# Overlapping windows copied by DMA alone: twelve staged batches in place of eleven, and packets of twice the size

## The chip, the cores and the metric

The kernel runs on one core of a Trainium2 chip. The metric is the device time of one execution in microseconds (us). A few repeated executions of the kernel before give its spread; one further execution was recorded by the hardware profiler.

## The reference

```python
batch, length, dim = (32, 4096, 256)     # float32
window_size, stride = 64, 32
n_windows = (length - window_size) // stride + 1      # 127
for i in range(n_windows):
    result[:, i] = x[:, i * stride : i * stride + window_size]
```

Nothing is computed: the result is a copy. Cut each batch of `x` into 128 blocks of 32 rows; a block is 32 x 256 x 4 = 32,768 bytes. Window `w` of a batch is block `w` followed by block `w+1`, 65,536 bytes in all. So every block but the first and the last of a batch appears twice in the result: as the first half of window `w` and as the second half of window `w-1`. The input has 134.2 MB, the result 32 x 127 x 65,536 bytes = 266.3 MB.

## The kernel before, in words

No compute engine does any work. There are two ways for a window to get into the result.

**Direct.** `Copier.windows` (L42 to L57, the DMA at L48) copies whole windows from DRAM to DRAM. Overlapping blocks are read twice. `max_dma_last_dim` sets the size of one packet: 32,768 bytes (`DIRECT`), so a window is two packets. With `half` 0 or 1 the DMA copies only the first or the second half of each of its windows.

**Staged.** `Copier.load` (DMA at L60) brings a whole batch, 128 blocks, into an SBUF tile of 128 partitions, one block each. `Copier.store` (DMA at L72) writes the tile twice: as the first halves and as the second halves of the windows. Here a block is read from DRAM once and written twice. Packets are 16,384 bytes (`IN`, `OUT`). A batch has 128 blocks but only 127 windows, so each of the two stores has one block too many; it lands in the half window next door, in the neighbouring batch, and that window is written again later. The last staged batch (number 30) avoids this by storing in four DMAs, of 112, 15, 15 and 112 rows (L99).

Three queues feed the same DMA engines:

- **ACT's queue** (`ring_s`) carries the staged batches 1, 4, ..., 28 and 30, eleven in all. `Staging.run` (L109 to L116) issues six loads into six tiles, then twelve stores, then five loads, then the last stores. A load into a used tile waits for both stores of that tile.
- **SP's queue** (`ring_d`) carries 7 groups of 16 windows, 112 windows, of each of the 21 other batches (L171 to L183). A counter (`share`, `turns`) decides for each group whether it goes as one DMA of whole windows or as two DMAs of halves.
- **GpSimd's queue** (`ring_r`, called POOL in the profile) carries the remaining 15 windows of each direct batch, among them those that a staged neighbour spills into. It starts when the group marked `near`, the third from the end of SP's list, has landed (L187), and waits for the stores of each neighbour before its DMA (L189 to L192).

At the end SP waits for all three (L193 to L195). A DMA tells its semaphore of the landing through packets of 4 bytes; these are records of their own in the trace.

Of the kernel before, what the change touches and what calls it, by code (L numbers as in the profile page):

```python
# [6 lines left out]


DIRECT, IN, OUT = 32768, 16384, 16384
PIECES = (32768,)  # L10


class Copier:


    def __init__(self, nc, tc, x, out, B, L, D, W, S, n_win):
        assert W == 2 * S and L % S == 0
        self.nc, self.tc, self.x, self.out = nc, tc, x, out
        self.B = B
        self.blk = S * D  # L20
        self.nb = L // S
        self.nw = n_win
        self.total = 0
        self.done = tc.alloc_semaphore("done")
        self.last = tc.alloc_semaphore("last")
        self.last_total = 0

    def xap(self, block, dims):
        return bass.AP(self.x.tensor, self.x.offset + block * self.blk, dims)

    def oap(self, elem, dims):
        return bass.AP(self.out.tensor, self.out.offset + elem, dims)

    def count(self, dma):
        dma.then_inc(self.done, 16)
        self.total += 16

    def count_last(self, dma):
        dma.then_inc(self.last, 16)
        self.last_total += 16  # L40

    def windows(self, q, b, w0, n, half=None, piece=DIRECT, count=None):  # L42

        blk = self.blk
        size = 2 * blk if half is None else blk
        off = blk if half else 0
        (count or self.count)(
            q.dma_start(  # L48
                out=self.oap((b * self.nw + w0) * 2 * blk + off, [[2 * blk, n], [1, size]]),
                in_=bass.AP(  # L50
                    self.x.tensor,
                    self.x.offset + (b * self.nb + w0) * blk + off,
                    [[blk, n], [1, size]],
                ),
                max_dma_last_dim=piece,
            )
        )  # L57

    def load(self, q, t, b):
        return q.dma_start(  # L60
            out=t[:, :], in_=self.xap(b * self.nb, [[self.blk, self.nb], [1, self.blk]]),
            max_dma_last_dim=IN,
        )

    def store(self, q, t, b, half, p0=0, n=None):

        blk = self.blk
        n = self.nb if n is None else n  # L70
        w = b * self.nw + p0 - half
        return q.dma_start(  # L72
            out=self.oap(w * 2 * blk + half * blk, [[2 * blk, n], [1, blk]]),
            in_=t[p0 : p0 + n, :],
            max_dma_last_dim=OUT,
        )


class Staging:


    def __init__(self, c, pool, dtype, batches, bufs):
        self.c, self.batches = c, batches
        self.tiles = [pool.tile([128, c.blk], dtype, name=f"xb{i}") for i in range(bufs)]
        self.loaded = [c.tc.alloc_semaphore(f"loaded{i}") for i in range(bufs)]
        self.stored = [c.tc.alloc_semaphore(f"stored{i}") for i in range(bufs)]

    def load(self, q, g):
        n, i = divmod(g, len(self.tiles))
        if n:  # L90
            q.wait_ge(self.stored[i], 32 * n)
        self.c.load(q, self.tiles[i], self.batches[g]).then_inc(self.loaded[i], 16)

    def store(self, q, g):
        n, i = divmod(g, len(self.tiles))
        q.wait_ge(self.loaded[i], 16 * (n + 1))
        if g == len(self.batches) - 1:

            for half, p0, rows in ((0, 0, 112), (0, 112, 15), (1, 1, 15), (1, 16, 112)):  # L99
                self.c.count_last(self.c.store(q, self.tiles[i], self.batches[g], half, p0, rows))  # L100
            return
        for half in (0, 1):
            self.c.store(q, self.tiles[i], self.batches[g], half).then_inc(self.stored[i], 16)

    def wait_stored(self, q, g):
        n, i = divmod(g, len(self.tiles))
# [12 lines left out]
@with_exitstack  # L119
def kernel(  # L120
    ctx: ExitStack,
    tc: tile.TileContext,
    x: bass.AP,
    window_size: bass.AP,
    stride: bass.AP,
    out: bass.AP,
):
    nc = tc.nc
    W, S = int(window_size), int(stride)
    B, L, D = x.shape  # L130
    n_win = (L - W) // S + 1
    assert out.shape == (B, n_win, W, D)
    c = Copier(nc, tc, x, out, B, L, D, W, S, n_win)
    staged = [*range(1, B - 3, 3), B - 2]
    direct = [b for b in range(B) if b not in staged]
    pool = ctx.enter_context(tc.tile_pool(name="xb", bufs=1))
    st = Staging(c, pool, x.dtype, staged, 6)
    ring_d, ring_s = nc.sync, nc.scalar
    spilled = staged[:-1]

    waits = {b: [g for g, n in enumerate(spilled) if abs(n - b) == 1] for b in direct}
    per, loads, stores = 6, 6 * 17, 34

    def first(b):
        return 0 if b - 1 not in spilled else 8 if len(waits[b]) == 2 else 15

    def rest_parts(b):
        if len(waits[b]) == 2:
            return [(0, 8), (120, 7)]
        return [(0 if b - 1 in spilled else 112, 15)]  # L150

    soft = tc.alloc_semaphore("soft")
    soft_total = 0

    near = tc.alloc_semaphore("near")

    def mark(dma):
        dma.then_inc(near, 16)

    def count_soft(dma):  # L160
        nonlocal soft_total
        dma.then_inc(soft, 16)
        soft_total += 16

    with tc.tile_critical():  # L165
        st.run(ring_s)

        turns = share = 0
        rests = []
        todo = 7 * len(direct)  # L170
        for b in direct:  # L171
            for j in range(7):
                at = turns % (loads + per * stores)
                share += 9 if at < loads else 3
                if share >= 12:
                    share -= 12
                    turns += 4
                    c.windows(ring_d, b, first(b) + 16 * j, 16, 0)
                    c.windows(ring_d, b, first(b) + 16 * j, 16, 1, count=mark if todo == 3 else None)
                else:  # L180
                    turns += 3
                    c.windows(ring_d, b, first(b) + 16 * j, 16, count=mark if todo == 3 else None)
                todo -= 1  # L183
            rests.append(b)

        ring_r = nc.gpsimd
        ring_r.wait_ge(near, 16)  # L187
        for i, b in enumerate(sorted(rests, key=lambda b: max(waits[b], default=0))):
            for g in waits[b]:  # L189
                st.wait_stored(ring_r, g)  # L190
            for w, n in rest_parts(b):
                c.windows(ring_r, b, w, n, None, PIECES[i % 1], count_soft)  # L192
        ring_d.wait_ge(c.done, c.total)  # L193
        ring_d.wait_ge(soft, soft_total)
        ring_d.wait_ge(c.last, c.last_total)  # L195


# [33 lines left out]
```

## Time and profile before

| | |
|---|---|
| median of 10 executions | 755.43 us (754.38 to 757.5) |
| profiled execution, its own time | 755.94 us |
| span of the profiled execution | 754.2 us |
| data moved by the DMA engines | 313.16 MB in 18,092 packets |
| DRAM read / written | 220.92 MB / 266.99 MB |
| SP's queue (q1) | 8,080 packets, 154.15 MB |
| ACT's queue (q10) | 9,002 packets, 138.35 MB |
| POOL's queue (q0) | 1,008 packets, 20.65 MB |

The span is the time between the first and the last instruction that the profiler saw on the core. The bytes of the DMA engines count each packet once; the DRAM bytes count what is read and what is written, so a direct packet counts in both and a staged one in one of them. The DMA share of a stretch is the mean busy share of the core's 16 DMA engines; it can be slightly above 1, because an engine's next packet starts a few ns before the last one's end. "Start" and "took" of every packet stand in the trace, with its queue and size, but not the engine that moved it.

### The profile page before, as it was taken

The page shows a single profiled execution, that of the slowest core. Times are in us where ns is not written, and L with a number is a line of the kernel's source. Part 1 is how long each engine was busy: PE and PEld are TensorE (multiplying, and loading weights), DVE is VectorE, ACT ScalarE, POOL GpSimd, SP SyncE. Part 2 cuts the span into 40 slices and gives each one's busy share as a digit, 9 for nine tenths or more (in the row PEclk, how much of TensorE's full clock was granted, in tenths as well). Part 3 has the DMA queues.
Part 4 walks back from the last instruction along what each step waited for, and adds up shares of the span by engine and source line. Part 5 has one row for each costly group of instructions (what it writes and reads, how often), then busy time and mean ns, then how long its engine had stood idle before and what let it go on. Part 6 is the DMA issues. An engine that isn't in the chain of part 4 may idle for free.

```text
span 754.2 us, 321 instructions
## 1 busy us (share of the span) xinstructions
POOL 12.4 (2%) x25
## 2 busy tenths in 40 slices
POOL 0000000000000000000000000000000000050000
DMA  9999999999999999999999999999999999999995
GB/s 370 422 426 416 428 423 418 432 421 417 424 424 417 410 428 414 421 420 420 428 423 398 428 422 428 433 421 434 424 427 423 417 423 423 421 425 423 407 411 220
DMA packets 18092, 313.16 MB, mean 415 GB/s; under 512 B 4312, under 2 KB 4312, under 8 KB 4312
## 3 DMA queue, kind: packets, MB, share of 16 engines
q1 hardware_dynamic: 8080, 154.15, 48.5%
q10 hardware_dynamic: 9002, 138.35, 44.0%
q0 software_dynamic: 1008, 20.65, 6.8%
q14 instruction: 2, 0.02, 0.0%
HBM read 220.92 MB, written 266.99 MB: 647 GB/s over the span
## 4 chain that ended last, share of the span: by engine, by line
another core or an unknown queue 91%; POOL 2%; issue 0%; POOLq 0%; SPq 0%
POOL out_dram L48 2%; POOLq L226 0%; SPq L165 0%; POOLq L107 0%
## 5 line engine op out<-in xcount | busy, mean ns | idle before, releaser
L48 POOL DMA_DIRECT2D out_dram<-in_x_dram x21 | 12.2, 586 | 683.6 <-DMA out_dram<-in_x_dram 662.4
L212 POOL MEMSET const-float32-0.0<- 128x1 f32 x1 | 0.1, 93 | 0.2 <-issue 0.2
L212 POOL MEMSET const-bfloat16-1.0<- 128x1 bf16 x1 | 0.1, 96 | 0.0
L212 POOL MEMSET const-float32-1.0<- 128x1 f32 x1 | 0.1, 93 | 0.0
L212 POOL MEMSET const-uint8-127<- 128x1 uint8 x1 | 0.1, 93 | 0.0
## 6 DMA issues: line engine op xcount, KB each, us to landing
out_dram<-in_x_dram SPq DMA_DIRECT2D x83, 1024.0 KB, 98.3
out_dram<-xb ACTq DMA_DIRECT2D x20, 4096.0 KB, 140.1
out_dram<-in_x_dram SPq DMA_DIRECT2D x128, 512.0 KB, 92.1
xb<-in_x_dram ACTq DMA_DIRECT2D x11, 4096.0 KB, 126.2
out_dram<-in_x_dram POOLq DMA_DIRECT2D x21, 960.0 KB, 46.5
out_dram<-xb ACTq DMA_DIRECT2D x2, 3584.0 KB, 127.7
out_dram<-xb ACTq DMA_DIRECT2D x2, 480.0 KB, 113.7
```

What stands on the lines that cost most here:

```text
L48: q.dma_start(out=self.oap((b * self.nw + w0) * 2 * blk + off, [[2 * blk, n], [1, size]]), in_=bass.AP(self.x.tensor, self.x.offset + (b * ...
L212: nc = _bacc.Bacc("TRN2", target_bir_lowering=False, num_devices=1)
```

## The change

- Packets are twice as large: 65,536 bytes direct (a window is one packet) and 32,768 bytes through SBUF (a block is one packet).
- Twelve batches are staged in place of eleven, 0, 3, 6, 9, 11, 14, 17, 20, 22, 25, 28 and 31, and 20 are direct. All stores have 128 partitions. Batch 0 is loaded one block later (blocks 1 to 128) and batch 31 one block earlier, so that their spilled halves fall into a direct neighbour and not outside the result. The first half of the first window of batch 0 and the second half of the last window of batch 31, which this leaves out, are two small direct DMAs with packets of 2,048 bytes.
- Direct groups are always whole windows. About every eleventh DMA on SP's queue has 32 windows in place of 16.
- On POOL's queue the remainders of 19 direct batches come in parts of 15, or of 8 and 7, windows. Of the last direct batch (30) come 4 windows, then 9 windows by `columns`, which cuts each block into 8 pieces of 4,096 bytes so that every one of 16 engines gets the same. Two more windows go by `columns` on SP's queue after the last staged batch has been stored.

```diff
-DIRECT, IN, OUT = 32768, 16384, 16384
-PIECES = (32768,)
+DIRECT, IN, OUT = 65536, 32768, 32768
...
+    def columns(self, q, b, w0, n):
+
+        part = self.blk // 8
+        row = [1, part]
+        return q.dma_start(
+            out=self.oap((b * self.nw + w0) * 2, [[part, 16], [2 * self.blk, n], row]),
+            in_=self.xap(b * self.nb + w0, [[part, 16], [self.blk, n], row]),
+        )
...
-        if g == len(self.batches) - 1:
-
-            for half, p0, rows in ((0, 0, 112), (0, 112, 15), (1, 1, 15), (1, 16, 112)):
-                self.c.count_last(self.c.store(q, self.tiles[i], self.batches[g], half, p0, rows))
-            return
         for half in (0, 1):
-            self.c.store(q, self.tiles[i], self.batches[g], half).then_inc(self.stored[i], 16)
+            self.c.store(q, self.tiles[i], self.batches[g], half, self.shift(g)).then_inc(self.stored[i], 16)
...
-    staged = [*range(1, B - 3, 3), B - 2]
+    staged = [0, 3, 6, 9, 11, 14, 17, 20, 22, 25, 28, 31]
...
+    st = Staging(c, tc, pool, x.dtype, staged, 6, {0: -1, B - 1: 1})
...
-        turns = share = 0
-        rests = []
-        todo = 7 * len(direct)
         for b in direct:
-            for j in range(7):
-                at = turns % (loads + per * stores)
-                share += 9 if at < loads else 3
-                if share >= 12:
-                    share -= 12
-                    turns += 4
-                    c.windows(ring_d, b, first(b) + 16 * j, 16, 0)
-                    c.windows(ring_d, b, first(b) + 16 * j, 16, 1, count=mark if todo == 3 else None)
-                else:
-                    turns += 3
-                    c.windows(ring_d, b, first(b) + 16 * j, 16, count=mark if todo == 3 else None)
-                todo -= 1
-            rests.append(b)
-
-        ring_r = nc.gpsimd
+            w = 0 if b - 1 not in staged else 8 if b + 1 in staged and b + 1 < B - 1 else 15
+            wend = w + 112
+            while w < wend:
+                share += 11
+                n = 16
+                if share >= 120 and w + 32 <= wend:
+                    share -= 120
+                    n = 32
+                todo -= n // 16
+                count(c.windows(ring_d, b, w, n), near if todo in (2, 2 - n // 16 + 1) and total[near] == 0 else done)
+                w += n
+                if todo <= 7 and not singles:
+                    singles = True
+                    count(c.windows(ring_d, B - 1, c.nw - 1, 1, 1, 2048), done)
+                    if 0 in staged:
+                        count(c.windows(ring_d, 0, 0, 1, 0, 2048), done)
+
         ring_r.wait_ge(near, 16)
...
+        for i, b in enumerate(direct[:-1]):
+            for g, n in enumerate(staged):
+                if abs(n - b) == 1:
+                    st.wait_stored(ring_r, g)
+            parts = [(0, 15)] if b - 1 in staged else [(112, 15)]
+            if b - 1 in staged and b + 1 in staged:
+                parts = [(0, 8), (120, 7)]
+            for w, n in parts:
+                count(c.windows(ring_r, b, w, n, None, pieces[i % len(pieces)]), rest)
+
+
+        count(c.windows(ring_r, last, 112, 4), rest)
+        count(c.columns(ring_r, last, 116, 9), rest)
+        st.wait_stored(ring_d, len(staged) - 1)
+        count(c.columns(ring_d, last, 125, 2), done)
+        for sem in (done, near, rest):
+            ring_d.wait_ge(sem, total[sem])
```

Built, the changed kernel has 132 DMAs on SP's queue (before 211), 36 on ACT's (35) and 23 on POOL's (21).

More of the change, by code (lines that the diff above doesn't have):

```diff
@@ L6, with __init__ @@
 from concourse._compat import with_exitstack
-DIRECT, IN, OUT = 32768, 16384, 16384
-PIECES = (32768,)
+DIRECT, IN, OUT = 65536, 32768, 32768
 class Copier:
-    def __init__(self, nc, tc, x, out, B, L, D, W, S, n_win):
+    def __init__(self, x, out, B, L, D, W, S, n_win):
         assert W == 2 * S and L % S == 0
-        self.nc, self.tc, self.x, self.out = nc, tc, x, out
+        self.x, self.out = x, out
         self.B = B
@@ L22, in __init__ @@
         self.nw = n_win
[L23 to L26, printed above, removed]
     def xap(self, block, dims):
         return bass.AP(self.x.tensor, self.x.offset + block * self.blk, dims)
[L31 to L40, printed above, removed]
@@ L42, in windows @@
-    def windows(self, q, b, w0, n, half=None, piece=DIRECT, count=None):
-        blk = self.blk
[L45 to L56, printed above, removed]
-        )
@@ L59, in load, with oap, windows @@
-    def load(self, q, t, b):
+    def oap(self, half_window, dims):
+        return bass.AP(self.out.tensor, self.out.offset + half_window * self.blk, dims)
+    def windows(self, q, b, w0, n, half=None, piece=DIRECT):
+        blk = self.blk
+        row = [1, 2 * blk if half is None else blk]
+        h = half or 0
+        return q.dma_start(
+            out=self.oap((b * self.nw + w0) * 2 + h, [[2 * blk, n], row]),
+            in_=self.xap(b * self.nb + w0 + h, [[blk, n], row]),
+            max_dma_last_dim=piece,
+        )
@@ L60, in load @@
+    def columns(self, q, b, w0, n):
+        part = self.blk // 8
+        row = [1, part]
         return q.dma_start(
-            out=t[:, :], in_=self.xap(b * self.nb, [[self.blk, self.nb], [1, self.blk]]),
+            out=self.oap((b * self.nw + w0) * 2, [[part, 16], [2 * self.blk, n], row]),
+            in_=self.xap(b * self.nb + w0, [[part, 16], [self.blk, n], row]),
+        )
+    def load(self, q, t, b, shift):
+        return q.dma_start(
+            out=t[:, :],
+            in_=self.xap(b * self.nb - shift, [[self.blk, self.nb], [1, self.blk]]),
@@ L62, in load, with store @@
             max_dma_last_dim=IN,
         )
[L65 to L71, printed above, removed]
+    def store(self, q, t, b, half, shift):
+        w = b * self.nw - half - shift
         return q.dma_start(
-            out=self.oap(w * 2 * blk + half * blk, [[2 * blk, n], [1, blk]]),
-            in_=t[p0 : p0 + n, :],
+            out=self.oap(2 * w + half, [[2 * self.blk, self.nb], [1, self.blk]]),
+            in_=t[:, :],
@@ L79, with __init__, shift @@
 class Staging:
-    def __init__(self, c, pool, dtype, batches, bufs):
-        self.c, self.batches = c, batches
+    def __init__(self, c, tc, pool, dtype, batches, bufs, shifts):
+        self.c, self.batches, self.shifts = c, batches, shifts
         self.tiles = [pool.tile([128, c.blk], dtype, name=f"xb{i}") for i in range(bufs)]
-        self.loaded = [c.tc.alloc_semaphore(f"loaded{i}") for i in range(bufs)]
-        self.stored = [c.tc.alloc_semaphore(f"stored{i}") for i in range(bufs)]
+        self.loaded = [tc.alloc_semaphore(f"loaded{i}") for i in range(bufs)]
+        self.stored = [tc.alloc_semaphore(f"stored{i}") for i in range(bufs)]
+    def shift(self, g):
+        return self.shifts.get(self.batches[g], 0)
     def load(self, q, g):
@@ L91, in load @@
             q.wait_ge(self.stored[i], 32 * n)
-        self.c.load(q, self.tiles[i], self.batches[g]).then_inc(self.loaded[i], 16)
+        self.c.load(q, self.tiles[i], self.batches[g], self.shift(g)).then_inc(self.loaded[i], 16)
     def store(self, q, g):
@@ L132 @@
     assert out.shape == (B, n_win, W, D)
-    c = Copier(nc, tc, x, out, B, L, D, W, S, n_win)
-    staged = [*range(1, B - 3, 3), B - 2]
+    c = Copier(x, out, B, L, D, W, S, n_win)
+    staged = [0, 3, 6, 9, 11, 14, 17, 20, 22, 25, 28, 31]
     direct = [b for b in range(B) if b not in staged]
     pool = ctx.enter_context(tc.tile_pool(name="xb", bufs=1))
[L137 to L153, printed above, removed]
-    near = tc.alloc_semaphore("near")
[L157 to L163, printed above, removed]
+    st = Staging(c, tc, pool, x.dtype, staged, 6, {0: -1, B - 1: 1})
@@ L165, with count @@
+    ring_d, ring_s, ring_r = nc.sync, nc.scalar, nc.gpsimd
+    done = tc.alloc_semaphore("done")
+    near = tc.alloc_semaphore("near")
+    rest = tc.alloc_semaphore("rest")
+    total = {done: 0, near: 0, rest: 0}
+    def count(dma, sem):
+        dma.then_inc(sem, 16)
+        total[sem] += 16
+    todo = 7 * len(direct)
+    share, singles = 0, False
     with tc.tile_critical():
         st.run(ring_s)
-        turns = share = 0
-        rests = []
-        todo = 7 * len(direct)
         for b in direct:
-            for j in range(7):
-                at = turns % (loads + per * stores)
-                share += 9 if at < loads else 3
-                if share >= 12:
-                    share -= 12
-                    turns += 4
-                    c.windows(ring_d, b, first(b) + 16 * j, 16, 0)
-                    c.windows(ring_d, b, first(b) + 16 * j, 16, 1, count=mark if todo == 3 else None)
-                else:
-                    turns += 3
-                    c.windows(ring_d, b, first(b) + 16 * j, 16, count=mark if todo == 3 else None)
-                todo -= 1
-            rests.append(b)
@@ L186 @@
-        ring_r = nc.gpsimd
-        ring_r.wait_ge(near, 16)
[L188 to L195, printed above, removed]
+            w = 0 if b - 1 not in staged else 8 if b + 1 in staged and b + 1 < B - 1 else 15
@@ new lines @@
+        ring_r.wait_ge(near, 16)
+        pieces = (65536,)
+        last = B - 2
+        for i, b in enumerate(direct[:-1]):
[7 more added lines that the diff above has]
+                count(c.windows(ring_r, b, w, n, None, pieces[i % len(pieces)]), rest)
```

## The prediction

> **What bounds the kernel now.** The page first: no engine computes, so its slices and the DMA queues are all there is. A packet of 4 bytes is the count towards a semaphore.
>
> ```profile
> DMA  9999999999999999999999999999999999999995
> DMA packets 18092, 313.16 MB, mean 415 GB/s; under 512 B 4312, under 2 KB 4312, under 8 KB 4312
> q1 hardware_dynamic: 8080, 154.15, 48.5%
> q10 hardware_dynamic: 9002, 138.35, 44.0%
> q0 software_dynamic: 1008, 20.65, 6.8%
> HBM read 220.92 MB, written 266.99 MB: 647 GB/s over the span
> ```
>
> The three shares add to 99.3%: the 16 DMA engines are full from start to end but for the last slice. So the time is the sum of packet times over 16, plus the two ends. Next the stretches (columns: from:to, length, POOL busy, clock, DMA share, GB/s moved):
>
> ```profile
> 20.00:140.00 120.00, 0.00 (x0) 1.00 1.00 422
> 140.00:400.00 260.00, 0.00 (x0) 1.00 1.01 421
> 415.00:540.00 125.00, 0.00 (x0) 1.00 1.00 427
> 545.00:660.00 115.00, 0.00 (x0) 1.00 1.01 422
> 680.00:720.00 40.00, 1.16 (x2) 1.00 1.01 417
> 720.00:740.00 20.00, 0.00 (x0) 1.00 1.02 393
> 740.00:745.00 5.00, 0.00 (x0) 1.00 0.89 321
> 745.00:751.00 6.00, 0.00 (x0) 1.00 0.33 142
> 751.00:754.20 3.20, 0.00 (x0) 1.00 0.00 0
> ```
>
> Engines are just as busy at 393 as at 427 GB/s: packets get longer. ACT's queue loads in the first and third of these rows and stores in the second and fourth; POOL's direct remainders run in the rows after. Last, the end of the chain of waits:
>
> ```profile
> 175.31 487.25 another core or an unknown queue
> 662.85 11.07 POOL out_dram L48 x19
> 673.93 20.93 another core or an unknown queue
> 695.15 1.16 POOL out_dram L48 x2
> ```
>
> POOL issues in two bursts and is done at 696; what remains until 751 is DMA.
>
> **Reading packets.** In the trace's packet records the commonest 32,768-byte packet takes 1,213 ns (direct or not), the 16,384-byte one 611 ns, the 4-byte one 9 ns. The difference of the first two is 602 ns for 16,384 bytes: 27.2 bytes per ns, and 9 ns on top. Neighbours overlap: between 20 and 740 us all durations sum to 3.5 ns per packet more than 16 engines have, so a packet costs 5.5 ns beyond its bytes. What a packet takes over that I call **stall**. It sums to 19.4 us per engine: 7.4 on q1, 8.9 on q10, 3.1 on q0. By stage: 0.8 before 20 us, 2.1% in the first loads, 2.5% in the first stores, 1.4 us at the changeover (400 to 415), 1.0% in the second loads, 2.1% in the second stores, 3.5% and 9.4% in the two rows with POOL.
>
> The span is then: 313.16 MB / (16 x 27.2) = 719.6; packets 18,092 x 5.5 ns / 16 = 6.2; stall 19.4; start 1.9 (engines idle in the first 10 us); uneven end 3.5 (five engines stop near 744.5, the last at 750.8, the mean is 747.3); landing 0.4 and the program's end 3.0. Sum 754.0 for 754.2.
>
> **What the Trainium skill says.** "DMA: Bandwidth & Descriptors", Where 436 GB/s comes from: 16 ports of 32 bytes at 850 MHz, 435.2 GB/s; the slope of 27.2 bytes per ns per engine agrees. "HBM Reference", Specifications, says that a core alone is bounded by its DMA engines and not by the per-core share of DRAM; 647 GB/s of reads and writes over the span agrees, though the stalls show that DRAM is not free. "DMA: Bandwidth & Descriptors", Queues, rings and completion order: each engine takes turns among its queues, a packet at a time. The trace agrees if a 4-byte packet counts as a turn: q1 had 8,080 / 16 = 505 turns by 671 us, when q10 had had 514. Its section on the semaphore increment says that 15 rows spread over 15 engines, on POOL from a moving cursor; 315 windows over 16 engines give 11 of them 20 and 5 of them 19, and five do stop first.
>
> **The change, part by part.**
>
> *Bytes.* One direct batch less, one staged more. Direct: 20 x 127 windows = 166.5 MB (before 174.8). Staged: 12 batches x 3 x 4.19 = 151.0 MB (before 138.4). With the two small ones 317.5 MB, +4.4 MB: a staged batch crosses the engines three times, a direct one twice. 317.5 / 435.2 = 729.6 us, **+10.0**. Nothing hides this, since the engines are full. DRAM traffic falls instead: read 216.8 and written 267.2, 484 for 488 MB.
>
> *Packets.* Direct 2,240 + 289, staged 4,608, small ones 32 + 32 + 144; semaphore packets 132 x 16 on q1, 36 x 16 on q10, 23 x 18 on q0 (378 / 21 = 18 in the trace). Together 10,447: x 5.5 / 16 = 3.6, **-2.6**. The trace has no 65,536-byte packet; by the line above it takes 2,418 ns. If it were cut in two, the 2,529 come twice: +0.9. No reason makes it cheaper than the bytes allow.
>
> *Turns.* q1 has 140 direct, 2 small and 131 semaphore packets per engine, 273 turns; q10 has 36 x 9 = 324. So q1 ends with 51 turns of q10 left, at 1.9 + (140 x 2.418 + 273 x 8/9 x 1.213) + small packets, some 635 us without stalls. POOL then brings 18 direct, 26 semaphore and 9 small packets, 53 turns: it stays level with q10. Its gates: the remainders next to batch 28 (27 and 29) wait for the last stores but two, 18 turns from q10's end; what is ahead of them is 37 turns, what ACT has before that is 33 and a few while q1 ends. So POOL waits little, and q10's packets cover it. ACT's own waits (a second load waits for both stores of its tile, 12th included) are covered by the loads already queued, 9 turns each.
>
> *Stall.* In the trace stores stall more when more engines are on direct packets: by stretches of 1 us in both store stages, 0 to 1.7% with 6 to 8 of 16 engines on direct, 1.7 to 2.2% with 8 to 9, 3.1 to 3.7% with 9 to 10. The mean there is 9.1, since SP's list has mostly whole windows (three turns for 64 KB). After, SP has two turns for 64 KB, against 8/9 x 32 KB per turn of ACT; direct time is 140 x 2.418 of 338.5 + 294.4, so 8.6 engines in all stages. I take 2.0% and 1.8% for the stores (-0.4 of a point), and the old 2.1% and 1.0% for the loads, which had 8.5 engines. Stages, from 54 and 108 turns of 2.32 us: 126, 251, 126, 130. That is 2.6 + 5.0 + 1.3 + 2.3 = 11.2. With POOL: direct 44 us of 100, 7 engines, 2.5% (between the store stages' 1.5 and the 4.9 that this stage had at 7 to 8): 2.5. Start 0.8, changeover 1.1 (1.4 before). **15.6, -3.8**. Bounds: 9 (all stages as clean as the second loads' 1.0%, ends kept) and 21 (nothing eases, longer packets add a little). Stall events of 50 to 200 ns hit 14% of q1's packets and 8% of q10's of half the length: they go with time, not with packet count, so doubling a packet saves none by itself.
>
> *End.* 289 windows over 16 are 18 and one over, so the evenness gains, but the engines still drift: of the 11 with equal load the last stopped 2.4 us after their mean. Uneven end 2.5, **-1.0**. New: SP waits for the last store (sixth tile, second use) before the last two windows. Behind it on SP are only the final waits. Nothing covers it: issue to first packet 1.1 (ACT's first load), two packets of 4,096 bytes and reading latency 0.6, and its own landing 0.4, hand-over 0.1: **+2.2**. It is 0 if POOL ends later by that much, at most 4 (POOL's issue to its first packet under load was 4.3). The two small direct DMAs cost 0.2, within rounding.
>
> Sum: 729.6 + 3.6 + 15.6 + 1.9 + 2.5 + 2.2 + 0.4 + 3.0 = 758.8, against 754.2: +4.6. The profiled execution took 755.94, 1.7 over its span; the median is 0.5 below that. So 755.4 + 4.6 = **760.0**.
>
> **The rivals.**
> 1. *DRAM relief wins: faster.* Fewer direct bytes and less write-plus-read at once let the stores run as clean as the second loads. For: 427 GB/s in 415:540, and the slope above. Against: that stage hardly wrote from SBUF, the first loads stalled 2.1% with the same mix, and written bytes do not fall. Without stall the sum is 743.2; with 8.5 it gives 751.7, a median of 752.9. It decides when stalls fall below 9.5, half of now.
> 2. *The two cancel: no change.* Stall 11, or 13 with POOL covering the last copy: 755.4.
> 3. *Long packets jam, or an engine is late: slower still.* Stall 20 and one engine with a 65,536-byte packet (2.4) at the end: 765.6, median 766.8. For: 720:740 shows how far a crowd of direct packets goes. Against: there POOL's direct share rises, after it falls.
> 4. *The change doesn't do what it says: 64 KB packets are cut in two.* Then q1 has 413 turns against 324, q10 ends first, and its last 89 turns (29 windows of 2.43 us) and POOL's 44 us are direct alone. At the 9.4% of 720:740 that is 10.8 us of stall for some 5 there now, and 0.9 for packets: 767.
>
> **How the numbers follow.** About 0.2% is what a measurement of this kernel tells from no change: 1.5 us. My forecast has 0.50, rival 1 0.22, rival 2 0.14, rivals 3 and 4 together 0.14. So faster 0.22, same 0.14, slower 0.64. The stall's bounds (9 to 21) and the end's (0 to 4) give 751.5 to 766; the forecast's own range is 757 to 763.
>
> **What would show it.** After: 317.5 MB in about 10,450 packets, q1 147, q10 151, q0 19.5 MB; commonest packets 2,418 and 1,213 ns; store stages at 424 GB/s or so, the POOL stage above 420; q1 ending near 645, q10 last but for some 128 KB on q1. I am wrong if the stall is below 10 us, if the 65,536-byte packets take less than their bytes at 27.2, or if q10 or q0 runs alone at the end for over 5 us.

## The result, and the profile after

The changed kernel takes 767.94 us (median of 9 executions, 765.72 to 771.27) against 755.38 us before (median of 32): a ratio of 1.0166 (95% interval 1.0152 to 1.0179), 1.7% slower. The direction was forecast, the size was not: +12.6 us for +4.6, outside the range of 757 to 763.

The same parts of the page, for the changed kernel's profiled execution (own time 766.79 us):

```profile
span 765.0 us, 247 instructions
...
DMA  9999999999999999999999999999999999999992
GB/s 370 418 430 413 423 421 418 430 437 418 440 424 430 421 433 423 435 428 425 437 398 423 425 416 437 416 420 433 432 427 435 416 440 432 420 439 423 403 395 97
DMA packets 10465, 317.54 MB, mean 415 GB/s; under 512 B 3119, under 2 KB 3119, under 8 KB 3327
...
q10 hardware_dynamic: 5184, 151.00, 46.7%
q1 hardware_dynamic: 4416, 147.01, 45.1%
q0 software_dynamic: 864, 19.53, 6.0%
...
HBM read 216.86 MB, written 267.19 MB: 633 GB/s over the span
```

Bytes and packets are those of the forecast. The three shares add to 97.8% of a span of 765.0, that is 748 us of work per engine; before they were 99.3% of 754.2, 749 us. **The engines did no more work than before.** What was added is idle time, and the last slice says where: 97 GB/s, where the kernel before still moved 220. Its line:

```profile
GB/s 370 422 426 416 428 423 418 432 421 417 424 424 417 410 428 414 421 420 420 428 423 398 428 422 428 433 421 434 424 427 423 417 423 423 421 425 423 407 411 220
```

The stretches of the changed kernel at the end (from:to, length, POOL busy, clock, DMA share, GB/s):

```profile
640.00:700.00 60.00, 9.91 (x19) 1.00 1.00 429
700.00:720.00 20.00, 0.00 (x0) 1.00 0.95 411
720.00:740.00 20.00, 2.12 (x4) 1.00 0.93 402
740.00:745.00 5.00, 0.00 (x0) 1.00 0.90 384
745.00:750.00 5.00, 0.00 (x0) 1.00 0.52 224
750.00:755.00 5.00, 0.00 (x0) 1.00 0.33 142
755.00:760.00 5.00, 0.00 (x0) 1.00 0.07 29
760.00:765.00 5.00, 0.00 (x0) 1.00 0.10 26
```

A share of 0.95 and 0.93 means that about one of 16 engines has nothing to do from just after 700; 0.52, 0.33 and 0.07 mean eight, five and one still working. The chain of waits (start, length, what) has POOL issuing in three bursts in place of two:

```profile
175.40 468.36 another core or an unknown queue
...
652.93 30.77 another core or an unknown queue
683.70 0.28 issue
683.98 1.03 POOL out_dram L34 x2
685.02 39.83 another core or an unknown queue
724.85 0.28 issue
725.12 1.55 POOL out_dram L34 x3
```

Its last gate opens at 724.85, when the slowest engine's part of the store of batch 28 lands.

For every run below the same sum is made from the packet records as in the prediction: bytes at 27.2 per ns, 5.5 ns a packet, stall (what packets take beyond that), idle at the start, **uneven end** (idle time from 640 us to the last packet, mean of 16 engines, without SP's last copy), and the rest (last copy, landing, program's end; 3.3 to 3.6 where there is no last copy or it is covered). All in us; the sums come within 0.9 of the spans.

| run | span | bytes | packets | stall | start | uneven | rest |
|---|---|---|---|---|---|---|---|
| before | 754.2 | 719.6 | 6.2 | 19.4 | 2.2 | 3.6 | 3.4 |
| predicted for after | 758.8 | 729.6 | 3.6 | 15.6 | 1.9 | 2.5 | 5.6 |
| after | 765.0 | 729.6 | 3.6 | 12.8 | 2.1 | 12.0 | 5.4 |
| no_last_copy | 763.5 | 729.3 | 3.6 | 13.5 | 2.2 | 11.6 | 3.5 |
| pool_32k | 767.5 | 729.6 | 3.7 | 22.4 | 2.2 | 6.1 | 3.5 |
| pool_columns | 768.6 | 729.6 | 5.1 | 23.7 | 2.1 | 4.8 | 3.4 |
| parts_8_7 | 808.3 | 729.6 | 3.8 | 15.9 | 2.1 | 52.1 | 4.9 |
| before_pool64 | 757.4 | 719.6 | 6.1 | 18.2 | 2.1 | 8.3 | 3.4 |
| twelve_small | 752.0 | 729.6 | 6.8 | 6.2 | 2.3 | 3.1 | 4.8 |
| pool64_small | 762.0 | 729.6 | 6.7 | 7.7 | 2.2 | 10.6 | 6.0 |
| staged_32k | 758.6 | 729.6 | 3.9 | 15.2 | 2.2 | 4.5 | 3.5 |
| no_pairs | 762.2 | 729.6 | 3.7 | 10.6 | 2.2 | 12.7 | 3.6 |
| eleven_large | 769.0 | 719.5 | 3.3 | 36.1 | 2.2 | 4.6 | 3.3 |
| twelve_small_no_wait | 752.0 | 729.4 | 6.8 | 7.6 | 2.2 | 2.8 | 3.5 |

One term is far from its forecast: the uneven end, 12.0 for 2.5.

### The profile page after: what moved, and what is told of

Its sections match the earlier page's. It is cut to its first block, busy times and chain, and to the rows that moved or that the text cites. A ratio compares the mean times of both kernels' runs of the same rounds, so it can differ in the third digit from the quotient of the medians.

```text
span 765.0 us, 247 instructions
## 1 busy us (share of the span) xinstructions
POOL 12.2 (2%) x27
## 4 chain that ended last, share of the span: by engine, by line
another core or an unknown queue 93%; POOL 2%; issue 0%; POOLq 0%; SPq 0%
POOL out_dram L34 1%; POOL out_dram L44 0%; POOLq L211 0%; SPq L140 0%; POOLq L94 0%
```

## Experiments on the uneven end

The trace does not name the engine of a packet, but a staged store's semaphore counts land one per engine. For ACT's last two stores in the changed kernel the first landings are at 695.6 and 705.7 us, then 727.0, up to 759.5. One engine did nine turns (eight packets of 1.213 us and a count) in 10.1 us: it had ACT's packets to itself, with none from POOL. Before, no engine stands out.

**pool_32k**: POOL's rows as two packets.

```diff
-        pieces = (65536,)
+        pieces = (32768,)
```

> The changed kernel with the remainders on POOL's queue in packets of 32,768 bytes, two a window, as before; all else as changed. In the changed kernel's packet records the engines are as busy in sum as before (748.1 for 748.5 us each), stall fell to 12.7 us, and the loss is an uneven end: one engine runs ACT's packets alone from 665 to 706 us, about ten others end at 743 to 756, the last at 759.6. Theory A, placement: with one 64 KB row per window POOL's DMAs of 15, 8, 7 and 4 rows all begin at the same engine, so the low engines get up to 22 windows and one gets none or few; before, with two packets a row, the start moved on. Then this run spreads evenly and the idle time before the end falls from 11.8 to 3 to 5 us: span 757 to 760, some 7 us faster than changed. Rival B, gates: the idle comes from POOL waiting for late stores (issues at 684 and 725 us); it stays, and the span stays within 2 us of 765. Rival C, parts: the parts of 8, 7 and 4 rows are what is uneven, whatever the packet; stays at 763 to 766.

Measured: 767.71 us, ratio 1.0160 (1.0137 to 1.0183), span 767.5. The early engine is gone: ACT's last two stores land from 723.0 to 750.8 us on all engines. The uneven end fell from 12.0 to 6.1. But stall rose by 9.6, most of it after 640 us, where POOL's queue has more turns and outlasts ACT's by 14 us (last packets at 764.0 and 749.7 us). The stretches of this run:

```profile
640.00:700.00 60.00, 10.80 (x19) 1.00 0.99 411
700.00:740.00 40.00, 2.27 (x4) 1.00 1.00 404
740.00:750.00 10.00, 0.00 (x0) 1.00 1.04 393
750.00:755.00 5.00, 0.00 (x0) 1.00 0.91 310
```

Engines are busy now (1.00 where there was 0.95 and 0.93) but move no more bytes: 404 for 411 and 402. So the span does not tell the three theories apart, and the net gain that theory A promised did not come; only the landings speak for it. That called for a run with a large effect.

**parts_8_7**: the changed kernel with every remainder of 15 windows as 8 and 7.

```diff
-            parts = [(0, 15)] if b - 1 in staged else [(112, 15)]
+            parts = [(0, 8), (8, 7)] if b - 1 in staged else [(112, 8), (120, 7)]
```

> The changed kernel with each remainder of 15 windows on POOL's queue as a DMA of 8 and one of 7 windows, rows still one packet of 65,536 bytes. The run with 32 KB packets on POOL made the one early engine vanish (ACT's last stores landed at 738 to 751 us on all engines, against 705 to 759), but lost the gain to stall. This run tests the placement itself. Theory A, every DMA of 64 KB rows begins at the same engine: the first seven engines get two windows of every batch, 38 or so, the eighth 19, the other eight none; the slowest engine then has 16 to 17 windows more than in the changed kernel (22), 17 x 2.42 = 41 us: span near 800 us. Rival, the start moves on with each DMA, and the uneven end has another cause: 18 windows each, span 750 to 766.

Measured: 810.33 us in one execution, span 808.3, where one start at the same engine gave 800 and a moving start at most 766. The page's slices:

```profile
DMA  9999999999999999999999999999999999955442
GB/s 386 417 420 427 405 422 422 438 418 428 429 412 438 418 435 438 420 425 431 386 418 412 422 417 427 423 433 428 428 417 430 436 430 427 414 219 225 201 191 104
```

From the 36th slice on, 707 us, the share is 5 tenths and less: half of the engines work or fewer. The landings of ACT's last two stores are split as theory A has it: eight engines land them by 698.6 and 708.5 us, one at 720.6 and 737.3, and seven from 742.1 and from 761.7 on. This settles the placement: **DMAs from POOL with rows of one 65,536-byte packet all begin at the same engine.** Counted out for the changed kernel: its parts of 15, 8, 7 and 4 windows, all begun at one engine, give four engines 22 windows, three 21, one 19, seven 17 and one none. The mean is 18.06; the excess of the slowest, 3.9 x 2.42 = 9.5 us, is what the uneven end has over the forecast. The part of 4 is too small to matter; 15 of 16 and 8 and 7 do it. Whether it is the size of 65,536 bytes or the one packet in a row that changes the placement, no run tells: pool_32k changed both.

**pool64_small** and **before_pool64** put such rows, and nothing else, into kernels that were even: the twelve staged batches with small packets (below), and the kernel before. The edit of pool64_small, against twelve_small, and then that of before_pool64, against the kernel before:

```diff
-        pieces = (32768,)
+        pieces = (65536,)
```

```diff
-PIECES = (32768,)
+PIECES = (65536,)
```

> The run of twelve staged batches with small packets (span 752.0, stall 6.2 us, uneven end 3.1), with POOL's remainders alone in rows of 65,536 bytes. Theory A (one start for 64 KB rows): the uneven end grows by what it did in the changed kernel, up to 9 us, less what the fewer turns of POOL take off; span 756 to 761, and one engine has ACT's packets alone once SP's queue has ended. Rival, long packets on the other two queues made the end uneven: 752 to 753.

> The kernel before with nothing changed but the packets on POOL's queue: rows of 65,536 bytes in 21 DMAs of 15 windows. If all of them begin at the same engine, 15 engines get 21 windows each and one none, where before they had 19 or 20: one or two windows more, 2.4 to 4.9 us, and one engine runs ACT's packets alone; span 757 to 760. If they rotate: 752 to 754.5.

Measured: pool64_small 764.54 us, 1.0121 (1.0096 to 1.0146), span 762.0, 10.0 over its parent. before_pool64 759.41 us, 1.0059 (1.0039 to 1.0078), span 757.4, +3.2. Their stretches, first pool64_small, then before_pool64:

```profile
700.00:720.00 20.00, 0.00 (x0) 1.00 0.94 397
720.00:740.00 20.00, 2.25 (x4) 1.00 0.93 395
```

```profile
700.00:720.00 20.00, 1.03 (x2) 1.00 0.96 396
720.00:740.00 20.00, 0.00 (x0) 1.00 0.95 384
```

Again the missing share, some 0.06, is one engine in 16 without work. In before_pool64 by the same count fifteen engines have 21 windows and one none, which moves the end less than the changed kernel's mixed parts. Uneven end 10.6 and 8.3, for 3.1 and 3.6 with rows of two packets.

**pool_columns**: evenness by construction, each window cut over all 16 engines.

```diff
-                count(c.windows(ring_r, b, w, n, None, pieces[i % len(pieces)]), rest)
+                count(c.columns(ring_r, b, w, n), rest)
...
-        count(c.windows(ring_r, last, 112, 4), rest)
-        count(c.columns(ring_r, last, 116, 9), rest)
+        count(c.columns(ring_r, last, 112, 13), rest)
```

> The changed kernel with every remainder on POOL's queue cut by columns, so that each of 16 engines gets 4,096 bytes of each half window piece and the same sum, by construction; the gates are as changed. Costs: 289 windows in 4,096-byte packets take 16 x 159 ns for 2,418, so 289 x 126 ns / 16 = 2.3 us more; and q0 has some 320 turns of which only 50 go beside ACT's, so it runs alone at the end for about 40 us, direct packets on all engines, with perhaps 2 to 4 us of stall. Theory A (placement): the uneven end of 11.8 us falls to about 3, net 757 to 761. Rival B (gates): engines wait as before, 767 or more. If A holds here and in the run with 32 KB packets, the parts of 8, 7 and 4 rows are to blame only as far as they all begin at one engine.

Measured: 770.30 us, 1.0196 (1.0181 to 1.0212), span 768.6. Uneven end 4.8, so the gates alone don't make it; but 10.1 us of stall on POOL's queue, mostly while it runs alone after ACT's end (22% between 720 and 751). I had put 2 to 4 on that, too little by 6 or more, and the run's total went to the rival's number for another reason.

**no_last_copy**: what SP's last two windows cost; these two windows are left out.

```diff
         st.wait_stored(ring_d, len(staged) - 1)
-        count(c.columns(ring_d, last, 125, 2), done)
```

> The changed kernel without SP's last copy of two windows after the last store (these two windows keep the spilled blocks); SP still waits for that store. Measured in the changed kernel's trace: last store's landing at 759.5, last copy's landing at 761.9. All theories: 2.2 to 2.6 us less than changed, span near 762.5; if the copy were covered by something, 0.

Measured: 766.82 us, 1.0151 (1.0128 to 1.0175), span 763.5. The rest falls from 5.4 to 3.5: 1.9 us, where 2.2 was forecast.

## Experiments on the stall

**twelve_small**: the changed kernel's batches with the packets of before.

```diff
-DIRECT, IN, OUT = 65536, 32768, 32768
+DIRECT, IN, OUT = 32768, 16384, 16384
...
-                share += 11
+                share += 86
                 n = 16
-                if share >= 120 and w + 32 <= wend:
-                    share -= 120
-                    n = 32
-                todo -= n // 16
...
+                todo -= 1
+                sem = near if todo == 2 else done
+                if share >= 100:
+                    share -= 100
+                    count(c.windows(ring_d, b, w, n, 0), done)
+                    count(c.windows(ring_d, b, w, n, 1), sem)
+                else:
+                    count(c.windows(ring_d, b, w, n), sem)
...
-        pieces = (65536,)
+        pieces = (32768,)
```

> The changed kernel's twelve staged batches with the packets of before: 32,768 bytes direct (also on POOL), 16,384 through SBUF, and SP's groups as pairs of halves in 86 of 100 cases, so that q1 has some 543 turns for 612 of q10 and direct packets hold 8.2 to 8.4 of 16 engines. It tells what packet size does to the stall with the share of direct packets kept. Stall from the share of direct packets (my prediction's step): 12 to 14 us as in the changed kernel. Stall from packet size: 17 to 20. Packets cost 2.6 us more than changed; POOL's placement as before, uneven end 3 to 5. Share: span near 758. Size: near 763.

Measured: 753.51 us, ratio 0.9977 (0.9964 to 0.9990), span 752.0: **slightly faster than before.** Both theories missed the stall, 6.2 us for 12 to 14 or 17 to 20. The batches alone take it from 19.4 to 6.2 and so more than pay for their 10.0 us of bytes; the large packets then put 6.6 back. The stretches of this run, and after them the same of the changed kernel:

```profile
20.00:140.00 120.00, 0.00 (x0) 1.00 1.00 425
140.00:400.00 260.00, 0.00 (x0) 1.00 1.01 429
415.00:540.00 125.00, 0.00 (x0) 1.00 1.00 429
545.00:660.00 115.00, 5.31 (x9) 1.00 1.01 431
```

```profile
20.00:140.00 120.00, 0.00 (x0) 1.00 1.00 421
140.00:400.00 260.00, 0.00 (x0) 1.00 1.00 426
415.00:540.00 125.00, 0.00 (x0) 1.00 1.00 424
545.00:660.00 115.00, 8.88 (x17) 1.00 1.00 429
```

All rows have full engines; the rate is 2 to 5 GB/s apart, with fewer and larger packets on the slower side. The share of direct packets is 8.34 engines here and 8.55 there, so two runs asked which difference matters. Stall is compared between 20 and 640 us, away from the ends.

**staged_32k**: staged packets large, direct ones small; DMAs of 112 windows keep the share of turns.

```diff
-DIRECT, IN, OUT = 65536, 32768, 32768
+DIRECT, IN, OUT = 32768, 32768, 32768
...
-                share += 11
-                n = 16
-                if share >= 120 and w + 32 <= wend:
-                    share -= 120
-                    n = 32
+                n = 112 if b < B - 2 else 80 if todo == 7 else 16
...
-        pieces = (65536,)
+        pieces = (32768,)
```

> Which of the two packet sizes makes the stall: the changed kernel with direct packets of 32,768 bytes on SP and POOL and staged ones of 32,768 as changed. SP's DMAs have 112 windows (14 packets and one semaphore packet per engine), so that direct packets hold about 8.2 of 16 engines as in the runs compared. Stall between 20 and 640 us was 10.9 us in the changed kernel and 3.5 us with small packets on both. Theory S, staged packets of 32 KB (first of all the loads, where ACT's packets stall): 9 to 12 us here. Theory D, direct packets of 64 KB: 3 to 5 us. The end is not comparable: POOL's queue has some 50 turns left when q10 ends and runs alone.

Measured: 760.38 us in one execution, span 758.6; 3.9 us of stall between 20 and 640. So staged packets of 32,768 bytes are not the cause of the stall there, and neither are whole windows as against halves, at the 8.18 engines of this run. (At its end POOL's packets run alone, 9.5 us of stall on that queue.)

**no_pairs**: the changed kernel at nearly the share of direct packets of twelve_small (8.40 engines for 8.34).

```diff
-                share += 11
```

> The changed kernel with every DMA on SP's queue of 16 windows, none of 32: 140 packets and 140 semaphore packets per engine, so that packets of 65,536 bytes stand at a share of direct packets of 8.45 engines, near the 8.35 of the run with small packets (20 to 640 us: 3.5 us of stall) and below the changed kernel's 8.6 (10.9 us). If the stall comes from 64 KB direct packets: 8 to 10 us there. If from the 0.2 engines of share: 4 to 6. The end stays uneven, span 762 to 766.

Measured: 763.98 us in one execution, span 762.2; 8.9 us between 20 and 640, for 11.0 in the changed kernel and 3.4 in twelve_small. So most of the difference in stall goes with direct packets of 65,536 bytes, and about 2 us with the share; but five runs with the changed kernel's list in this stage lie between 11 and 14 us, so the 2 is not settled. What this stall is made of is taken up after the next run.

**eleven_large**: eleven batches with the large packets.

```diff
-DIRECT, IN, OUT = 32768, 16384, 16384
+DIRECT, IN, OUT = 65536, 32768, 32768
...
+            j = 0
+            while j < 7:
+                share += 8
+                n = 1
+                if share >= 13 and j < 6:
+                    share -= 13
+                    n = 2
...
```

> The kernel before, eleven staged batches, with packets of 65,536 bytes on SP's queue and 32,768 through SBUF, POOL's remainders in 32,768 as before; SP's groups are always whole windows, 56 pairs of groups as one DMA of 32 windows, so that q1 has 238 turns for q10's 299 and POOL fills the rest. Direct packets hold about 9.3 of 16 engines. Theory 1, long packets add some 6 us of stall whatever the batches (12.8 against 6.2 with twelve): stall 22 to 27, packets 3 us less, span 756 to 761. Theory 2, the stall depends on the share of direct packets alone: 20 to 22, span 752 to 755.

Measured: 771.49 us, 1.0235 (1.0175 to 1.0295), span 769.0. Stall 36.1, far above both theories; 27.4 of it between 20 and 640 with direct packets on 9.26 engines. Large packets and a large share add to more than each alone: at 8.4 engines large packets stalled 8.9, at 8.8 small ones 13.8 (before), at 8.3 small ones 3.4.

**What fills up between 20 and 640 us.** The packet records hold one more number. A direct packet is both read from DRAM and written to it, a staged one only one of the two. Counted so, DRAM read and wrote nearly the same in all thirteen kernels, 650 to 657 GB/s (645 to 662 in the single stages of loads and stores), while the engines moved 414 to 431, the less the more of the bytes were direct. Six of them:

| run | direct share of the bytes | moved, GB/s | DRAM read and written, GB/s |
|---|---|---|---|
| eleven_large | 58.2% | 414.2 | 655.4 |
| before | 55.3% | 422.0 | 655.5 |
| after | 53.7% | 425.5 | 653.8 |
| no_pairs | 52.6% | 427.0 | 651.5 |
| twelve_small | 52.3% | 429.1 | 653.6 |
| staged_32k | 51.1% | 430.5 | 650.3 |

Three more stretches: one of pool_columns with few direct packets (12% of the bytes), then one of pool_columns and one of staged_32k in which they go alone:

```profile
655.00:695.00 40.00, 2.77 (x5) 1.00 1.00 431
720.00:740.00 20.00, 0.00 (x0) 1.00 1.01 326
720.00:740.00 20.00, 0.00 (x0) 1.00 1.02 328
```

Alone, direct packets make 652 and 656 GB/s of DRAM traffic, twice what is moved: the same again. Where few bytes are direct, the engines moved 431 at a DRAM traffic of 482. The simplest reading is that DRAM traffic is the bound between 20 and 640 us, and that stall is the room between that bound and the engines' own 431. Then time saved on packets comes back as stall: no_pairs spends 2.7 us less on packets there than twelve_small, about half of the 5.5 us by which it stalls more. The other half is slightly more direct bytes and a DRAM rate 0.3% lower, and five runs with the changed kernel's list differ by more (650.3 to 653.8). So a cost of long direct packets in themselves is not shown. No run was made to test this reading, and it does not cover two stretches in which POOL's windows go in two packets beside ACT's stores: pool_32k from 690 to 740 us and eleven_large from 680 to 740 moved 404 and 394 GB/s with all engines busy, at a DRAM traffic of some 560.

**twelve_small_no_wait**: the faster version without the last copy.

```diff
-    st = Staging(c, tc, pool, x.dtype, staged, 6, {0: -1, B - 1: 1})
+    st = Staging(c, tc, pool, x.dtype, staged, 6, {0: -1})
...
+        if g == len(self.batches) - 1:
+
+            for half, p0, rows in ((0, 0, 112), (0, 112, 15), (1, 1, 15), (1, 16, 112)):
+                self.c.store(q, self.tiles[i], self.batches[g], half, 0, p0, rows).then_inc(self.last, 16)
+            return
...
-        count(c.columns(ring_r, last, 116, 9), rest)
-        st.wait_stored(ring_d, len(staged) - 1)
-        count(c.columns(ring_d, last, 125, 2), done)
+        count(c.columns(ring_r, last, 116, 11), rest)
+        ring_d.wait_ge(st.last, 64)
```

> The run of twelve staged batches with small packets, without the copy that waits for the last store: batch 31 is loaded unshifted and stored by 112, 15, 15 and 112 rows as the last batch of before, so that nothing of batch 30 has to be written after it; POOL's last columns copy has 11 windows for 9. The last copy cost 1.9 us in the changed kernel (765.0 with, 763.5 and 1.9 less between last packet and span's end without); stores of 15 rows leave one engine out, up to 1.2 us. Expected: span 749.5 to 751, a ratio of 0.994 to 0.997 to before. If POOL's queue ends last in any case, no gain over 752.0.

Measured: 753.60 us, 0.9983 (0.9974 to 0.9992), span 752.0: faster than before, and no gain over its parent. The rest fell from 4.8 to 3.5 as it should, but stall was 7.6 for 6.2 in this execution. Both versions beat the kernel before by some 0.2% and the changed kernel by nearly 2%.

## Why the prediction was wrong, step by step

- **Bytes** (+10.0) and **packets** (-2.6): as forecast, 729.6 and 3.6. The commonest 65,536-byte packet takes 2,418 ns, as its line said. But "nothing hides this", said of the bytes, did not hold: in twelve_small 13.2 us less of stall more than paid for them. I took the 647 GB/s of DRAM traffic as agreeing with engines that are the bound, and added bytes, packets and stall as if each stood for itself. That traffic is at nearly the same level in every kernel between 20 and 640 us; if it is the bound there, the three depend on each other.
- **Stall** (15.6, -3.8): 12.8. The direction was right and the size too small, and it was two effects in one: twelve batches alone bring 6.2, large packets add 6.6. What failed in it is to leave the stall as it was when packets double and to book the packets' 2.6 us as a gain beside it: by the reading above they came back as stall in the changed kernel, and some more with the larger share of direct packets. With POOL I took 2.5% and found 0.2% to 0.4% between 680 and 740, perhaps in part because fewer engines were at work.
- **End, uneven** (2.5): 12.0. This is the step that put the time outside the range. It read "289 windows over 16 are 18 and one over", and rests on the Trainium skill's moving start on POOL ("DMA: Bandwidth & Descriptors", the section on the semaphore increment). The kernel before agreed with it, with rows of two packets; parts_8_7 shows that it does not hold for rows of one 65,536-byte packet, and the measurement decides. The change made such rows out of POOL's DMAs, and I carried the evenness over from a shape that the trace showed to one that it did not show, without a bound for the case that the placement changes with it.
- **POOL's gates**: POOL did wait (30.8 and 39.8 us in the chain), and q10's packets did cover it on most engines, as said; the engine that had no window ran out of them at 705.7 us and then stood idle.
- **Last copy** (+2.2): 1.9 by no_last_copy. **Start and landing**: within 0.2.

That the kernel came out slower, as forecast, is luck: the batches, which were to make it slower, made it 2.2 us faster by themselves, and most of what made it slower was not in my sum.

The rivals: relief of the kind that rival 1 named was larger than I gave it, as twelve_small shows; with the large packets on top it could not decide. Rival 3 named a number close to the result (766.8), but by another mechanism: stall of 20 and one late packet, where it was stall of 12.8 and an engine four packets over the mean. Rival 4 did not occur: the packets are not cut.

From before to after in two measured steps: twelve batches -2.2 us of span (bytes +10.0, packets +0.6, stall -13.2, uneven end -0.5, rest +1.4); large packets +13.0 (packets -3.2, stall +6.6, uneven end +8.9, rest +0.6). Of the 13.0, POOL's rows alone make 10.0 (pool64_small), the large packets on the other two queues the remaining 3.0.

## What to carry to other kernels

When a kernel keeps its DMA engines full, compare the sum of the queues' shares first: equal work in a longer span means that some engines ended early, and no average over 16 shows which. The number of engines that a DMA is cut over is not enough; which engines it begins at decides when many DMAs have fewer rows than engines, and it can change with the shape of a row, so look at the landings of single engines after changing a packet size. Count also what DRAM reads and writes, not only what the engines move: here the first was at 650 to 657 GB/s in every kernel, and fewer and larger packets, with 5.5 ns each to save, moved no more in the same time.

## What the runs showed of the hardware

- POOL's DMAs of fewer than 16 rows (15, 8 and 7 here) spread evenly over time with rows of two 32,768-byte packets, and begin at one and the same engine with rows of one 65,536-byte packet: 752.0 and 762.0 us for the same kernel otherwise.
- Between 20 and 640 us DRAM read and wrote 650 to 657 GB/s in all thirteen kernels, while the engines moved 414 GB/s with 58% of the bytes direct and 431 with 51%. Direct packets alone on all engines ran at 326 to 328 GB/s (pool_columns and staged_32k between 720 and 740).
- Direct packets of 65,536 bytes moved no more than those of 32,768 at nearly the same share: 427.0 against 429.1 GB/s, with 8.9 against 3.4 us of stall in 620. Staged packets of 32,768 bytes did not raise the stall over 16,384 (3.9 us, at 8.2 engines).
- Open: pool_32k moved 404 GB/s with full engines in a stage where the changed kernel, uneven, moved 402 to 411 with 0.93 to 0.95; even placement gave more stall there, eleven_large had the like, and no run says why.
